# First tile's weight sums ahead of the norm, its stream sums on VectorE, modulation rows in halves with buffers of their own, and the feed-forward groups as 4 4 3 3 4 4

## The chip, the cores and the metric

The kernel runs on one core of a Trainium2 chip. The metric is the device time of one execution in microseconds, and of a kernel its median over several runs. The kernel before took 1985.98 us (three runs, 1985.26 to 1990.08).

The engines are named as in the profile: PE is TensorE (PEld its weight loads), DVE is VectorE, ACT is ScalarE, POOL is GpSimd, and SP is SyncE, whose queue issues nearly all transfers. Each engine works through its own list of instructions in order, and waits at an instruction until the semaphores it needs have come.

## The reference, cut to what matters

Two layers of a transformer trunk over 512 latent and 256 context tokens, width 1024, all in float32. Layer 0 is differential attention beside a gated DeltaNet, layer 1 neighbourhood attention. Each layer ends with a SwiGLU feed-forward block, and each half of a layer starts with an RMS norm that is modulated by rows computed from the conditioning vectors:

```python
m = silu_c @ ada_w[l] + ada_b[l]                      # 6 rows of 1024: shifts, scales, gates
hf = rms_norm(x, norm_ffn[l]) * (1.0 + sc_f) + sh_f   # the norm ahead of the feed-forward block
x = x + g_f * swiglu(hf, ffn_w_in[l], ffn_w_out[l])   # silu(h @ w_gate) * (h @ w_up) @ w_out
```

The hidden width is 2816, or 22 tiles of 128. The change is in the feed-forward block of layer 0 (768 tokens) and in the two norms around it. While that block runs, the kernel also computes the modulation rows of layer 1.

## The kernel before, in words

**Precision.** Every float32 product is three TensorE passes. An operand is split in two parts, `hi` (ACT rounds it, `ACTIVATE`) and `lo` (DVE subtracts, `TENSOR_TENSOR`), and `mm3` (L180) adds hi·hi, hi·lo and lo·hi in one PSUM bank.

**The block upwards.** Gate and up product of a hidden tile are computed together by Strassen's scheme in Winograd's form: seven products in place of eight, over the two halves of the 1024 input rows and over gate and up as the two halves of the columns. That needs sums of blocks on both sides.

On the weight side, `weights(t)` (L1503) loads the tile's gate part `g` and up part `u` (512 KB each) into the staging ring `st` (two buffers for the whole kernel, `wstage`), and POOL forms four sums in two buffers `ws` (L1508, L1509, L1512, L1513). ACT and DVE split `g`, the two sums and the last block `a22` (L1499, L1500).

On the stream side, the sums are formed once, by the norm object `NormS`. Its method `finish` normalises a third of the tokens (context, then two halves of the latents), `put` writes `hf`, and `half` forms the sums. `half(0)` splits `b11` and `b21`, which need only the first two thirds. `half(1)` forms T1 and T2 on DVE (L414, L416) and T3 and T4 on POOL (L420, L423), and splits these and `b22` (L399, L400).

For each tile `up` runs `b11`, `b21`, then T2, T1, then T3, `b22`, then T4: seven times twelve passes of 384 columns, 84 in all. It ends with `emit`, which writes the tile `mid`.

**The block downwards.** After each group of tiles (`GROUPS0`: 4 4 4 4 3 3), `down` multiplies the group's `mid` tiles with the output weights, one output channel tile after the other (eight, called channels below): a load of 256 KB (for four tiles), a split (L166, L167), and 24 passes per channel for a group of four, half of 256 and half of 512 columns, and two updates of `x` on DVE (L1579). In the last group, five of the channels are done third by third, so that the next norm can start on the first third. `mid` has five buffers, shared with the four `hf`.

**The modulation rows.** `ada_rows` (L277) computes three blocks of sixteen row sums. Per row tile it loads 512 KB through the same ring `st`, and DVE multiplies with a row of silu(c) and sums (L286): two instructions of 512 columns, and in the first block four, since it serves latents and context. One step (`ada_step`) is a row tile. It is called once a channel, and before every second tile from the second group on.

**The norm.** `acc` squares a channel tile on ACT (L322) and adds it to a running sum (L324). Tiles from `on_v` on are added on DVE, the others on POOL. `NORMS` has 5 for the norm ahead of this block (`n0f`) and 8 for the one behind it (`n1m`), that is, all on POOL. `finish` adds over partitions on PE (`sp`, L335), takes the inverse root in some fourteen small instructions (`rsqrt`, L194 to L206, nearly all on POOL), spreads it over the partitions on PE (`rb`, L341), and scales on DVE (L344).

**What sets the order.** The program is written in one sequence, and a scheduler lays it out on the engines by its own estimate of times. The order of an engine is therefore not that of the text.

Of the kernel before, what the change touches and what calls it, by code (L numbers as in the profile page):

```python
# [22 lines left out]
GROUPS = [(0, 6), (6, 5), (11, 6), (17, 5)]  # L23
GROUPS0 = [(0, 4), (4, 4), (8, 4), (12, 4), (16, 3), (19, 3)]
HALF = 384
# [8 lines left out]
ORDER = "vp0 out1 Ad0 Bd1 vp1 Bd2 Bd3 Ad1 Ad2 G2 G0 Ad3 G1 G3".split()  # L34
NORMS = dict(n0f=(5, 'G', (7,)), n1m=(8, 'G', (7,)), n1f=(4, 'G', ()))
FILL = dict(out1=2, Ad0=1, vp1=2, Ad2=1, G2=3, Ad3=1, G1=3)
# [90 lines left out]
def build(tc, a, out, dbg=None):  # L127
# [3 lines left out]
    with es:  # L131
# [145 lines left out]
        def ada_rows(l, b, ns, stage, cbc, junk):  # L277
            lab(f"ada{l}{b}")
            sc = ct(f"scal{l}{b}", [128, 2, 16])
            part = ct("adpart", [128, 2, 2, 16])  # L280
            for j in range(16):
                st = stage(a["ada_t"][l, 16 * b + j], 1024)
                for s in range(ns):
                    for i in range(2):
                        cs = slice(512 * i, 512 * i + 512)
                        r = V.scalar_tensor_tensor(  # L286
                            out=junk() if s < ns - 1 else st[:, cs], in0=st[:, cs], scalar=1.0, in1=cbc[:, s, cs],
                            op0=ALU.mult, op1=ALU.mult, accum_out=part[:, s, i, j:j + 1],
                        )
                        tc.add_manual_dep(r.ins, last_lo[0].name, after, reason="pace")  # L290
                yield 0, 0
            for s in range(ns):
                V.tensor_tensor(out=sc[:, s, :], in0=part[:, s, 0, :], in1=part[:, s, 1, :], op=ALU.add)
                V.tensor_tensor(out=sc[:, s, :], in0=sc[:, s, :], in1=ada_b[:, l, 16 * b:16 * b + 16], op=ALU.add)
            ada_names(l, b, sc, ns)
            yield 0, 0
# [65 lines left out]
        class NormS(Norm):  # L362
# [12 lines left out]
            def put(self, k, s, sl, t):  # L375
                if self.hf is None:
                    self.hf = [self.fp.tile([128, 2, 2, HALF], F32, name="hf", tag="mid", bufs=5) for _ in range(4)]
                d = self.hf[k // 2][:, k % 2]
# [24 lines left out]
            def half(self, i):  # L403
# [3 lines left out]
                if i == 0:  # L407
# [3 lines left out]
                    return  # L411
                t1 = [self.fp.tile([128, 1024], F32, name="t1", tag="ws", bufs=2)[:, 0:2 * HALF].rearrange("p (z n) -> p z n", z=2) for _ in range(2)]
                for q in range(2):
# [4 lines left out]
                for q in range(2):  # L418
                    self.split("T1", q, t1[q])
                    G.tensor_tensor(out=b(0, 1, q), in0=b(1, 1, q), in1=b(0, 1, q), op=ALU.subtract)  # L420
                for q in range(2):
                    self.split("T3", q, b(0, 1, q))
                    G.tensor_tensor(out=b(1, 0, q), in0=b(1, 0, q), in1=b(0, 0, q), op=ALU.subtract)  # L423
                for q in range(2):
# [196 lines left out]
def l0_mixer(kx, hi, lo, xes):  # L621
# [799 lines left out]
    kx.fp0 = kx.fpx.enter_context(tc.tile_pool(name="fp0", bufs=1))  # L1421
    kx.n0 = kx.NormS(x, 0, "f", kx.np, kx.gs, SEGS, kx.fp0)
    for q, (s, sl) in enumerate(SEGS):
        lab("out2")
# [43 lines left out]


def ffn0(kx, x, nm, next_norm):  # L1470
    tc, nc, a = kx.tc, kx.nc, kx.a
# [7 lines left out]
    with kx.fpx:  # L1479

        def adas():
            cbc = fp.tile([128, 2, 1024], F32, name="cbc", tag="cbc", bufs=1)
            DMA.dma_start(out=cbc, in_=a["cbc"])
            S.activation(out=cbc, in_=cbc, func=AF.Silu)
            junk = lambda: gs.tile([128, 512], F32, name="junk", tag="C")
            for b in range(3):
                yield from kx.ada_rows(1, b, 1 if b else 2, kx.wstage, cbc, junk)

# [14 lines left out]
        def weights(t):  # L1503
            g, u = (kx.wstage(a["wfi"][0, t, z], 1024) for z in range(2))
            a11, a12, a21, a22 = g[:, 0:512], g[:, 512:1024], u[:, 0:512], u[:, 512:1024]
            yield split(g, 1024)
            sa = fp.tile([128, 1024], F32, name="ws", tag="ws", bufs=2)
            G.tensor_tensor(out=sa[:, 0:512], in0=a21, in1=a22, op=ALU.add)  # L1508
            G.tensor_tensor(out=sa[:, 512:1024], in0=sa[:, 0:512], in1=a11, op=ALU.subtract)  # L1509
            yield split(sa, 1024)  # L1510
            sb = fp.tile([128, 1024], F32, name="ws", tag="ws", bufs=2)
            G.tensor_tensor(out=sb[:, 0:512], in0=a11, in1=a21, op=ALU.subtract)  # L1512
            G.tensor_tensor(out=sb[:, 512:1024], in0=a12, in1=sa[:, 512:1024], op=ALU.subtract)  # L1513
            yield split(sb, 1024)
            yield split(a22, 512, ("a22h", "a22l"))

# [65 lines left out]

        for gi, (t0, ng) in enumerate(GROUPS0):
            mids = [fp.tile([128, 2, 2, HALF], F32R, name="mid", tag="mid", bufs=5) for _ in range(ng)]
            for t in range(t0, t0 + ng):
                if gi and t % 2:
                    ada_step()
                lab(f"ffi0{gi}")
                for _ in up(t, mids[t - t0]):
                    pass  # L1590
            tail = 5 if gi == len(GROUPS0) - 1 else 0
# [365 lines left out]
```

## Time and profile before

| what | value |
|---|---|
| median of three runs | 1985.98 us |
| the profiled execution: its own time, its span | 1987.38 us, 1985.6 us |
| mean granted TensorE clock | 0.961 |
| PE busy | 1807.4 us, 91% of the span |
| DVE, ACT, POOL busy | 1239.4, 805.1, 380.0 us |
| the block of layer 0 with the norm behind it | 693 to 1300 us of the span |

Times in the profile count from the span's start. A row of a group view reads: line, engine, operation, output and inputs, shape, count, then busy time in us and mean duration in ns, then the engine's idle time just before these instructions and what ended it. A row of a timeline reads: start and duration in us, engine, line, operation, and in brackets the idle time before it with what ended it. A row of a table of stretches gives for each engine its busy time and, in brackets, the number of instructions, then the granted clock, the share of DMA engines that were busy and GB/s.

### The profile page before, as it was taken

How to read it: one execution, taken by the hardware profiler on the slowest of the kernel's cores; microseconds unless marked ns; L12 is line 12 of the kernel's file. 1: busy time of each engine (PE TensorE's matmuls, PEld its weight loads, DVE VectorE, ACT ScalarE, POOL GpSimd, SP SyncE). 2: the span in 40 equal slices, each digit the busy share in tenths (PEclk: the TensorE clock that was granted, in tenths of full speed). 3: DMA queues.
4: the chain of work that ended last, by engine and by line, in shares of the span. 5: the costliest groups of instructions: out<-in, count | busy, mean ns of one | idle time of the engine just before them, and what ended most of it. 6: DMA issues, size and time to landing. Idle time of an engine off the chain costs nothing.

```text
span 1985.6 us, 30314 instructions
## 1 busy us (share of the span) xinstructions
PE 1807.4 (91%) x11328; PEld 1625.1 (82%) x11328; DVE 1239.4 (62%) x2826; ACT 805.1 (41%) x1773; POOL 380.0 (19%) x449
## 2 busy tenths in 40 slices
PE   5978999798989939899999998889999989999999
PEld 3867889677878839798989897879999778888887
DVE  6556688776676677777767776656565663434333
ACT  3434554345664453141424232445555442222221
POOL 2132314431210063030413113321101020000000
PEclk8978999899999969999999999989999989999999
DMA  7556645647444602323243433311211213323232
GB/s 293 154 177 208 195 140 153 185 136 218 112 153 130 222 13 81 120 98 126 96 149 101 144 108 115 106 40 57 69 55 45 79 33 106 106 77 114 85 107 94
DMA packets 107522, 238.41 MB, mean 120 GB/s; under 512 B 11152, under 2 KB 50320, under 8 KB 106224
## 3 DMA queue, kind: packets, MB, share of 16 engines
q1 hardware_dynamic: 94848, 208.31, 32.9%
q0 software_dynamic: 4064, 14.38, 2.5%
q10 hardware_dynamic: 8464, 13.79, 2.0%
q8 instruction: 89, 1.46, 0.3%
q14 instruction: 57, 0.47, 0.1%
HBM read 203.44 MB, written 32.99 MB: 119 GB/s over the span
## 4 chain that ended last, share of the span: by engine, by line
PE 56%; DVE 15%; DMA 14%; POOL 5%; ACT 4%; issue 4%; SPq 0%; POOLq 0%; ACTq 0%; DVEq 0%
PE f L180 25%; PE d L180 17%; DMA st<-in_ada_t_dram 4%; DMA qkd<-ar 3%; PE o L180 3%; DMA st<-in_wfi_dram 2%; DVE st L286 2%; DVE wlo L1500 1%; PE vp L547 1%; PE sc L1762 1%; POOL ws L1508 1%; PE o L1787 1%; POOL ws L1512 1%; DVE ev L1536 1%; POOL ws L1509 1%
## 5 line engine op out<-in xcount | busy, mean ns | idle before, releaser
L166 ACT ACTIVATE whi<-st 128x1024 fp32r<-128x1024 f32 (+6 forms) x191 | 170.1, 892 | 451.7 <-PE f L180 195.6
L167 DVE TENSOR_TENSOR wlo<-st,whi 128x1024 fp32r<-128x1024 f32 (+6 forms) x191 | 196.4, 1029 | 158.3 <-ACT whi L166 155.8
L180 PE MATMUL d<-whi,hhi 128*128 128x256 f32 (+1 forms) x800 | 235.3, 296 | 20.1 <-ACT ar L211 13.3
L180 PE MATMUL d<-wlo,hhi 128*128 128x256 f32 (+1 forms) x800 | 233.3, 292 | 1.3 <-DVE wlo L167 1.3
L180 PE MATMUL d<-whi,hlo 128*128 128x256 f32 (+1 forms) x800 | 233.0, 293 | 0.2 <-DVE hlo L357 0.2
L180 PE MATMUL f<-hhi,whi 128*128 128x512 f32 (+2 forms) x632 | 229.6, 364 | 1.7 <-ACT hhi L356 1.0
L180 PE MATMUL f<-hlo,whi 128*128 128x512 f32 (+2 forms) x632 | 230.0, 364 | 0.2 <-DVE hlo L357 0.2
L180 PE MATMUL f<-hhi,wlo 128*128 128x512 f32 (+2 forms) x632 | 227.6, 362 | 0.0
L180 PEld LDWEIGHTS d<-whi,hhi 128*128 128x128 f32 x800 | 157.3, 197 | 26.4 <-ACT ar L211 14.6
L180 PE MATMUL f<-mid,whi 128*128 128x512 f32 (+1 forms) x644 | 159.0, 343 | 6.8 <-ACT whi L166 5.8
L180 PE MATMUL f<-v,whi 128*128 128x384 f32 x528 | 138.8, 344 | 27.1 <-ACT whi L1499 24.5
L180 PEld LDWEIGHTS d<-wlo,hhi 128*128 128x128 f32 x800 | 157.6, 197 | 2.5 <-DVE wlo L167 1.7
L180 PEld LDWEIGHTS d<-whi,hlo 128*128 128x128 f32 x800 | 157.0, 197 | 1.6 <-DVE hlo L357 0.4
L180 PEld LDWEIGHTS f<-hhi,whi 128*128 128x128 f32 x632 | 119.9, 190 | 15.8 <-ACT whi L1499 1.5
L180 PEld LDWEIGHTS f<-hlo,whi 128*128 128x128 f32 x632 | 120.3, 190 | 13.8 <-DVE hlo L357 0.5
L180 PEld LDWEIGHTS f<-hhi,wlo 128*128 128x128 f32 x632 | 119.7, 190 | 13.1
L180 PEld LDWEIGHTS f<-mid,whi 128*128 128x128 f32 x644 | 109.4, 192 | 23.8 <-ACT whi L166 9.8
L180 PEld LDWEIGHTS f<-v,whi 128*128 128x128 f32 x528 | 97.9, 194 | 30.3 <-ACT whi L1499 26.9
L180 PE MATMUL d<-hhi,whi 128*128 128x512 f32 (+1 forms) x304 | 107.9, 355 | 3.1 <-ACT cin L211 1.4
L180 PE MATMUL f<-mid,wlo 128*128 128x256 f32 (+1 forms) x322 | 106.1, 343 | 5.1 <-DVE wlo L167 5.0
L1508 POOL TENSOR_TENSOR ws<-st 128x512 f32<-128x512 f32 x22 | 32.5, 1476 | 383.3 <-DMA st<-in_wfi_dram 296.2
L180 PE MATMUL d<-hlo,whi 128*128 128x512 f32 (+1 forms) x304 | 105.8, 348 | 0.0
(410 smaller groups left out, 4319.6 us busy)
## 6 DMA issues: line engine op xcount, KB each, us to landing
st<-in_wfi_dram SPq DMA_DIRECT2D x88, 512.0 KB, 3.3
st<-in_ada_t_dram SPq DMA_DIRECT2D x48, 512.0 KB, 3.3
st<-in_ada_w_dram SPq DMA_DIRECT2D x32, 512.0 KB, 4.2
aw<-in_ada_dram SPq DMA_DIRECT2D x8, 1024.0 KB, 12.6
st<-in_wfo_dram SPq DMA_DIRECT2D x32, 256.0 KB, 3.4
st<-in_w1kv_dram SPq DMA_DIRECT2D x16, 512.0 KB, 3.2
aqT<-qkd SPq DMA_DIRECT2D x48, 128.0 KB, 3.2
st<-in_wfo_dram SPq DMA_DIRECT2D x16, 384.0 KB, 3.0
```

Of the source, the lines that this page charges most:

```text
L166: S.activation(out=hi, in_=st, func=AF.Copy)
L167: last_lo[:] = [V.tensor_tensor(out=lo, in0=st, in1=hi.bitcast(F32), op=ALU.subtract).ins]
L180: r = T.matmul(out=ps, lhsT=p, rhs=q, start=(c == 0), stop=(c == n - 1))
L286: r = V.scalar_tensor_tensor(out=junk() if s < ns - 1 else st[:, cs], in0=st[:, cs], scalar=1.0, in1=cbc[:, s, cs], op0=ALU.mult, op1=ALU. ...
L547: T.matmul(out=vp[i, s], lhsT=w[:, ws], rhs=h[k][:, sl], start=(k == 0 and q == 0), stop=(k == KT - 1 and q == 2),)
L1500: kx.last_lo[:] = [V.tensor_tensor(out=lo, in0=src, in1=hi.bitcast(F32), op=ALU.subtract).ins]
L1508: G.tensor_tensor(out=sa[:, 0:512], in0=a21, in1=a22, op=ALU.add)
L1509: G.tensor_tensor(out=sa[:, 512:1024], in0=sa[:, 0:512], in1=a11, op=ALU.subtract)
L1512: G.tensor_tensor(out=sb[:, 0:512], in0=a11, in1=a21, op=ALU.subtract)
L1536: V.tensor_tensor(out=out, in0=ps, in1=sb, op=ALU.add)
L1762: T.matmul(out=o, lhsT=lq[:, q], rhs=kv(lk), start=(i == 0), stop=(i == 2))
L1787: T.matmul(out=o, lhsT=lv[:, v, :], rhs=p, start=(n == 0 and i == 0), stop=(n == 5 and i == 2))
```

## The change

- **Weight sums of the first tile.** A new function `prep` holds the loads and the four POOL sums. For tile 0 it is called before the norm's loop and the result kept in `kx.prep0`. In group 0, the first part of tiles 0 and 1 (`b11`, `b21`) is recorded ahead of the rest of both.
- **Stream sums on VectorE.** T3 and T4 go from POOL to DVE. The buffer of T1 is no longer taken from `ws` but from that of the row `cbc`.
- **Modulation rows in halves.** A step is half a row tile (256 KB), and goes through a ring of its own, `ast`, with three buffers. Steps are taken after the first and second part of a tile from tile 2 on (in the last three groups after all three parts), and once a channel as before.
- **Norm behind the block.** `n1m` has 5 for 8: channel tiles 5, 6 and 7 are added on DVE.
- **Groups** 4 4 3 3 4 4, and four `mid` buffers for five.

```diff
-GROUPS0 = [(0, 4), (4, 4), (8, 4), (12, 4), (16, 3), (19, 3)]
+GROUPS0 = [(0, 4), (4, 4), (8, 3), (11, 3), (14, 4), (18, 4)]
-NORMS = dict(n0f=(5, 'G', (7,)), n1m=(8, 'G', (7,)), n1f=(4, 'G', ()))
+NORMS = dict(n0f=(5, 'G', (7,)), n1m=(5, 'G', (7,)), n1f=(4, 'G', ()))
...
             for j in range(16):
-                st = stage(a["ada_t"][l, 16 * b + j], 1024)
-                for s in range(ns):
-                    for i in range(2):
-                        cs = slice(512 * i, 512 * i + 512)
+                for i in range(2):
+                    cs = slice(512 * i, 512 * i + 512)
+                    st = stage(a["ada_t"][l, 16 * b + j, :, cs], 512)
+                    for s in range(ns):
...
-                yield 0, 0
+                    yield 0, 0
...
-                t1 = [self.fp.tile([128, 1024], F32, name="t1", tag="ws", bufs=2)[:, 0:2 * HALF].rearrange("p (z n) -> p z n", z=2) for _ in range(2)]
+                t1 = self.fp.tile([128, 2, 2, HALF], F32, name="t1", tag="cbc", bufs=1)
+                t1 = [t1[:, q] for q in range(2)]
...
-                    G.tensor_tensor(out=b(0, 1, q), in0=b(1, 1, q), in1=b(0, 1, q), op=ALU.subtract)
+                    V.tensor_tensor(out=b(0, 1, q), in0=b(1, 1, q), in1=b(0, 1, q), op=ALU.subtract)
...
-                    G.tensor_tensor(out=b(1, 0, q), in0=b(1, 0, q), in1=b(0, 0, q), op=ALU.subtract)
+                    V.tensor_tensor(out=b(1, 0, q), in0=b(1, 0, q), in1=b(0, 0, q), op=ALU.subtract)
...
     kx.n0 = kx.NormS(x, 0, "f", kx.np, kx.gs, SEGS, kx.fp0)
+    kx.prep0 = prep(kx, 0)
...
+def prep(kx, t):
+    G = kx.nc.gpsimd
+    g, u = (kx.wstage(kx.a["wfi"][0, t, z], 1024) for z in range(2))
+    a11, a12, a21, a22 = g[:, 0:512], g[:, 512:1024], u[:, 0:512], u[:, 512:1024]
+    sa, sb = (kx.fp0.tile([128, 1024], F32, name="ws", tag="ws", bufs=2) for _ in range(2))
+    G.tensor_tensor(out=sa[:, 0:512], in0=a21, in1=a22, op=ALU.add)
+    G.tensor_tensor(out=sa[:, 512:1024], in0=sa[:, 0:512], in1=a11, op=ALU.subtract)
+    G.tensor_tensor(out=sb[:, 0:512], in0=a11, in1=a21, op=ALU.subtract)
+    G.tensor_tensor(out=sb[:, 512:1024], in0=a12, in1=sa[:, 512:1024], op=ALU.subtract)
+    return g, u, sa, sb
...
+            def astage(src, n):
+                st = fp.tile([128, n], F32, name="ast", tag="ast", bufs=3)
+                DMA.dma_start(out=st, in_=src)
+                return st
+
             for b in range(3):
-                yield from kx.ada_rows(1, b, 1 if b else 2, kx.wstage, cbc, junk)
+                yield from kx.ada_rows(1, b, 1 if b else 2, astage, cbc, junk)
...
         for gi, (t0, ng) in enumerate(GROUPS0):
-            mids = [fp.tile([128, 2, 2, HALF], F32R, name="mid", tag="mid", bufs=5) for _ in range(ng)]
-            for t in range(t0, t0 + ng):
-                if gi and t % 2:
-                    ada_step()
-                lab(f"ffi0{gi}")
-                for _ in up(t, mids[t - t0]):
-                    pass
+            mids = [fp.tile([128, 2, 2, HALF], F32R, name="mid", tag="mid", bufs=4) for _ in range(ng)]
+            ups = [up(t, mids[t - t0]) for t in range(t0, t0 + ng)]
+            lab(f"ffi0{gi}")
+            if gi == 0:
+                for u in ups[0:2]:
+                    next(u)
+            for i, u in enumerate(ups):
+                for j, _ in enumerate(u):
+                    if t0 + i > 1 and (j or gi > 2):
+                        ada_step()
+                        lab(f"ffi0{gi}")
```

Where the scheduler puts it shows at three places. Up to the norm ahead of the block and behind the one after it, the lists of all engines are the same as before.

**POOL, around the norm ahead of the block.** `ssq` are the running sums of squares of the three thirds, `rs_y` and `rs_t` the inverse root, `ws` the weight sums, `st` the staged weights. Before, the four sums of tile 0 stand behind the last inverse root and among the stream sums:

```order
L206 TENSOR_TENSOR rs_y_7782<-rs_y_7782,rs_t_7783 128x2
L420 TENSOR_TENSOR hf_7511<-hf_7513,hf_7511 128x2x384
L420 TENSOR_TENSOR hf_7512<-hf_7514,hf_7512 128x2x384
L423 TENSOR_TENSOR hf_7513<-hf_7513,hf_7511 128x2x384
L1508 TENSOR_TENSOR ws_7920<-st_7883 128x512
L423 TENSOR_TENSOR hf_7514<-hf_7514,hf_7512 128x2x384
L1512 TENSOR_TENSOR ws_7956<-st_7881,st_7883 128x512
```

Now they stand at the head of the list, among the first squares, and two of tile 1's (`ws_7929`) inside the first third's inverse root:

```order
L1477 TENSOR_TENSOR ws_7400<-st_7398 128x512
L1479 TENSOR_TENSOR ws_7401<-st_7396,st_7398 128x512
L324 TENSOR_TENSOR ssq0_7414<-ssq0_7414,sq_7424 128x256
L1478 TENSOR_TENSOR ws_7400<-ws_7400,st_7396 128x512
L324 TENSOR_TENSOR ssq0_7414<-ssq0_7414,sq_7435 128x256
L1480 TENSOR_TENSOR ws_7401<-st_7396,ws_7400 128x512
```

```order
L206 TENSOR_TENSOR rs_y_7498<-rs_y_7498,rs_t_7499 128x2
L1477 TENSOR_TENSOR ws_7929<-st_7927 128x512
L200 TENSOR_TENSOR rs_t_7499<-rs_y_7498 128x2
L324 TENSOR_TENSOR ssq2_7708<-ssq2_7708,sq_7729 128x256
L1478 TENSOR_TENSOR ws_7929<-ws_7929,st_7925 128x512
L201 TENSOR_TENSOR rs_t_7499<-rs_t_7499,rs_v_7500 128x2
```

`ws_7929` takes the buffer of `ws_7400`, so it is written only after DVE has split that one.

**SP, the loads of the first group's channels.** `in_ada_t` are the modulation rows, `in_wfo` the output weights. Before, both take turns in `st`:

```order
L160 DMA st<-in_ada_t_dram 128x1024
L160 DMA st<-in_wfo_dram 128x512
L160 DMA st<-in_ada_t_dram 128x1024
L160 DMA st<-in_wfo_dram 128x512
L160 DMA st<-in_ada_t_dram 128x1024
```

Now the rows are half as long and go to `ast`, and `st` is left to the weights:

```order
L1503 DMA ast<-in_ada_t_dram 128x512 x2
L160 DMA st<-in_wfo_dram 128x512
L1503 DMA ast<-in_ada_t_dram 128x512
L160 DMA st<-in_wfo_dram 128x512
L1503 DMA ast<-in_ada_t_dram 128x512 x2
```

**POOL, the norm behind the block.** Before, the last squares of the second and third thirds stand between the steps of the first third's inverse root:

```order
L198 TENSOR_SCALAR rs_v_12735<-ms_12731 128x2
L324 TENSOR_TENSOR ssq1_12530<-ssq1_12530,sq_12854 128x256
L197 TENSOR_SCALAR rs_y_12733<-rs_y_12733 128x2
L324 TENSOR_TENSOR ssq2_12532<-ssq2_12532,sq_12927 128x256
L200 TENSOR_TENSOR rs_t_12734<-rs_y_12733 128x2
L324 TENSOR_TENSOR ssq2_12532<-ssq2_12532,sq_12941 128x256
L201 TENSOR_TENSOR rs_t_12734<-rs_t_12734,rs_v_12735 128x2
```

Now the first root runs through, and what is left of the squares follows it:

```order
L198 TENSOR_SCALAR rs_v_12815<-ms_12811 128x2
L197 TENSOR_SCALAR rs_y_12813<-rs_y_12813 128x2
L200 TENSOR_TENSOR rs_t_12814<-rs_y_12813 128x2
L201 TENSOR_TENSOR rs_t_12814<-rs_t_12814,rs_v_12815 128x2
L205 TENSOR_SCALAR rs_t_12814<-rs_t_12814 128x2
```

On PE, the first third's `sp` stood 27 passes of the block ahead of the end, and no pass stood between `rb` of the first third and `rb` of the second. Now 75 passes follow `sp`, 55 of them ahead of the first `rb` and 20 between the first and the second.

More of the change, by code (lines that the diff above doesn't have):

```diff
@@ L281, in ada_rows @@
             for j in range(16):
-                st = stage(a["ada_t"][l, 16 * b + j], 1024)
-                for s in range(ns):
-                    for i in range(2):
-                        cs = slice(512 * i, 512 * i + 512)
+                for i in range(2):
+                    cs = slice(512 * i, 512 * i + 512)
+                    st = stage(a["ada_t"][l, 16 * b + j, :, cs], 512)
+                    for s in range(ns):
                         r = V.scalar_tensor_tensor(
-                            out=junk() if s < ns - 1 else st[:, cs], in0=st[:, cs], scalar=1.0, in1=cbc[:, s, cs],
+                            out=junk() if s < ns - 1 else st, in0=st, scalar=1.0, in1=cbc[:, s, cs],
                             op0=ALU.mult, op1=ALU.mult, accum_out=part[:, s, i, j:j + 1],
@@ L376, in put @@
                 if self.hf is None:
-                    self.hf = [self.fp.tile([128, 2, 2, HALF], F32, name="hf", tag="mid", bufs=5) for _ in range(4)]
+                    self.hf = [self.fp.tile([128, 2, 2, HALF], F32, name="hf", tag="mid", bufs=4) for _ in range(4)]
                 d = self.hf[k // 2][:, k % 2]
@@ L1503, in weights @@
         def weights(t):
-            g, u = (kx.wstage(a["wfi"][0, t, z], 1024) for z in range(2))
-            a11, a12, a21, a22 = g[:, 0:512], g[:, 512:1024], u[:, 0:512], u[:, 512:1024]
+            g, u, sa, sb = kx.prep0 if t == 0 else prep(kx, t)
             yield split(g, 1024)
-            sa = fp.tile([128, 1024], F32, name="ws", tag="ws", bufs=2)
-            G.tensor_tensor(out=sa[:, 0:512], in0=a21, in1=a22, op=ALU.add)
-            G.tensor_tensor(out=sa[:, 512:1024], in0=sa[:, 0:512], in1=a11, op=ALU.subtract)
             yield split(sa, 1024)
-            sb = fp.tile([128, 1024], F32, name="ws", tag="ws", bufs=2)
-            G.tensor_tensor(out=sb[:, 0:512], in0=a11, in1=a21, op=ALU.subtract)
-            G.tensor_tensor(out=sb[:, 512:1024], in0=a12, in1=sa[:, 512:1024], op=ALU.subtract)
             yield split(sb, 1024)
-            yield split(a22, 512, ("a22h", "a22l"))
+            yield split(u[:, 512:1024], 512, ("a22h", "a22l"))
         cnt = [0]
```

## The prediction

> **What bounds the kernel now.** I read the page first, for the engine that bounds:
>
> ```profile
> PE 1807.4 (91%) x11328; PEld 1625.1 (82%) x11328; DVE 1239.4 (62%) x2826; ACT 805.1 (41%) x1773; POOL 380.0 (19%) x449
> ```
>
> PE does, so an edit is worth the PE time without progress that it removes. The lists of all engines differ only from the norm ahead of layer 0's feed-forward block to the norm behind it. So I cut that part, 693 to 1300 us, at its stages: norm, then upward and downward passes of each group in turn, then norm.
>
> ```profile
> core 0: us, PE busy (x) PEld busy (x) DVE busy (x) ACT busy (x) POOL busy (x), PEclk, DMA share, GB/s
> 693.00:742.40 49.40, 17.88 (x100) 16.27 (x99) 38.49 (x59) 29.49 (x60) 31.64 (x58) 0.69 0.03 11
> 742.40:799.10 56.70, 56.15 (x313) 55.33 (x314) 44.95 (x74) 21.23 (x31) 17.91 (x13) 0.97 0.25 81
> 799.10:840.20 41.10, 35.49 (x193) 28.60 (x192) 29.82 (x75) 5.90 (x9) 0.00 (x0) 1.00 0.40 133
> 840.20:903.10 62.90, 60.80 (x337) 59.83 (x338) 47.99 (x88) 22.70 (x34) 22.46 (x16) 0.97 0.28 93
> 903.10:943.00 39.90, 37.09 (x194) 31.50 (x193) 28.30 (x71) 7.02 (x11) 0.50 (x1) 0.91 0.39 132
> 943.00:1002.80 59.80, 58.87 (x338) 58.24 (x337) 42.11 (x72) 22.46 (x33) 20.46 (x16) 1.00 0.34 109
> 1002.80:1036.90 34.10, 33.70 (x194) 29.32 (x193) 24.21 (x53) 6.89 (x11) 0.32 (x1) 1.00 0.46 149
> 1131.10:1175.40 44.30, 43.98 (x253) 43.64 (x252) 31.17 (x58) 16.44 (x25) 13.98 (x11) 1.00 0.34 109
> 1175.40:1208.10 32.70, 27.15 (x146) 21.34 (x144) 23.44 (x54) 5.51 (x10) 0.00 (x0) 1.00 0.46 149
> 1208.10:1255.50 47.40, 46.19 (x252) 45.23 (x253) 32.42 (x56) 18.36 (x28) 16.19 (x12) 0.96 0.29 92
> 1278.90:1300.40 21.50, 7.65 (x47) 7.27 (x47) 8.57 (x23) 8.56 (x22) 14.48 (x39) 0.65 0.09 26
> ```
>
> The same work takes unequal times. Four tiles upwards cost 59.8 us at best (336 passes, 0.178 us each) and 62.9 in the second group. Eight channels downwards cost 34.1 us at best (4.26 a channel), but 41.1 and 39.9 in the first two groups. In the fifth group, three tiles need 44.3 us upwards, and downwards 32.7, where three quarters of 34.1 are 25.6; the sixth needs 47.4 upwards. The two norms take 49.4 and 21.5 us with little on PE.
>
> **Part 1: modulation rows.** The waits for PE and the transfers in the first group's channels:
>
> ```profile
> 790.64 3.31 DMA st<-in_ada_t_dram
> 797.00 3.34 DMA st<-in_ada_t_dram
> 803.90 3.44 DMA st<-in_ada_t_dram
> PE f L180 <- ACT whi L166: 5.8, 7, 1.2
> st<-in_ada_t_dram SPq DMA_DIRECT2D x7, 512.0 KB, 3.4
> st<-in_wfo_dram SPq DMA_DIRECT2D x8, 256.0 KB, 3.5
> L286 DVE SCALAR_TENSOR_TENSOR junk<-st,cbc 128x512 f32<-128x512 f32 x12 | 8.1, 717 | 4.7 <-DMA st<-in_ada_t_dram 4.7
> L286 DVE SCALAR_TENSOR_TENSOR st<-st,cbc 128x512 f32<-128x512 f32 x12 | 7.9, 688 | 0.0
> L1579 DVE SCALAR_TENSOR_TENSOR x<-f,scal,x 128x512 f32<-128x512 f32 x7 | 5.2, 746 | 0.0
> L167 DVE TENSOR_TENSOR wlo<-st,whi 128x512 fp32r<-128x512 f32 x6 | 4.1, 688 | 0.1
> L1579 DVE SCALAR_TENSOR_TENSOR x<-f,scal,x 128x256 f32<-128x256 f32 x8 | 3.8, 480 | 3.6 <-PE f L180 3.6
> L166 ACT ACTIVATE whi<-st 128x512 fp32r<-128x512 f32 x6 | 3.8, 632 | 26.3 <-DMA st<-in_wfo_dram 17.6 <-PE f L180 8.7
> ```
>
> A row tile starts every 6.4 to 6.9 us: 3.3 to 3.4 of landing, then two products of 717 and two of 688 ns before its buffer is free, 6.2 in all. Output weights take turns with it in the same queue, so they come at that pace, against PE's 4.26 a channel. PE lives off its three split buffers and then waits.
>
> Now `st` holds weights alone. A buffer turns in 3.5 + 0.63 + 0.69 = 4.8 us, two give a load every 2.4. A half row turns in 3.5 + 1.4 = 4.9, three give one every 1.6. VectorE needs 0.69 + 0.48 + 0.75 + 1.4 = 3.3 us a channel. All are under 4.26, so PE bounds again. The excess over the best is 41.1 − 34.1 = 7.0; 62.9 − 59.8 = 3.1; 39.9 − 34.1 = 5.8; 32.7 − 25.6 = 7.1; 47.4 − 44.3 = 3.1: **26.1 us**. The new order of groups is the same sum of parts.
>
> Not all comes back. I leave 1 us for each of five turns between groups, where the first load upwards still follows the last output weights, and 2 for the upward passes: the second group takes eight half steps for two whole ones, four more of 1.4 us on VectorE, 47.99 + 5.6 = 53.6 of 59.8. Gain **19**, bounds 8 (VectorE holds PE up) and 26. `mid` with four buffers costs nothing: the first write into a new one follows 60 passes (10.7 us) behind the last reader on PE. If that cover were gone, the price is those passes once a group.
>
> A rule of the Trainium skill speaks against halves: "DMA: Bandwidth & Descriptors", section "Rules for kernel authors", asks for transfers of 1 MiB and more. The rows bear it out in part, 256 KB landing no sooner than 512 (3.5 and 3.4 us). By that rule the sum would lose this part and more; its rival stands below.
>
> **Part 2: the norm ahead of the block and the first tiles.**
>
> ```profile
> 689.72 1.28 ACT L1484 ACT_TABLE_LOAD   x1
> 691.14 1.91 ACT L1484 ACTIVATE cbc<-cbc 128x2048 f32<-128x2048 f32 x1
> 693.44 1.56 POOL L324 TENSOR_TENSOR ssq<-ssq,sq 128x256 f32<-128x256 f32 x2 [5.05 <-ACT sq L322]
> 702.75 0.71 PE L341 MATMUL rb<-cst,rs_y 128*128 128x128 f32 x4 [3.02 <-POOL rs_y L206]
> 718.62 1.22 PE L341 MATMUL rb<-cst,rs_y 128*128 128x128 f32 x4 [1.77 <-POOL rs_y L206]
> 729.51 0.95 DVE L400 TENSOR_TENSOR hlo<-hf,hhi 128x768 fp32r<-128x768 f32 x1
> 730.38 2.56 DVE L400 TENSOR_TENSOR hlo<-t,hhi 128x768 fp32r<-128x768 f32 x1
> 739.30 1.97 POOL L1509 TENSOR_TENSOR ws<-ws,st 128x512 f32<-128x512 f32 x1
> 742.42 1.01 PE L180 MATMUL f<-v,whi 128*128 128x384 f32 x2 [18.56 <-ACT whi L1499]
> 752.26 1.29 POOL L1509 TENSOR_TENSOR ws<-ws,st 128x512 f32<-128x512 f32 x1
> ```
>
> PE stands 18.6 us for the split of tile 0's first sum, which POOL finishes at 739.30 + 1.97. That wait goes, but what is late next is the norm. POOL gets six sums ahead of the first `rb`: four of tile 0, two of tile 1, at 1.3 (alone) to 2.0 us (beside VectorE), 8 to 12 us. Its idle time there was 5.0 in one gap, mostly from the Silu of `cbc` with its table load (3.2 us on ACT), which moves away; the gap is now filled. Net 3 to 7 us late. Worse, tile 1's first sum stands in the first third's root and needs the buffer that VectorE frees; by the order of VectorE's list that split follows the last squares, at about 703. I take 7 (first `rb` from 702.8 to 710), and with the same steps behind it the last one too (725.6).
>
> Behind the last `rb`, VectorE has eight scalings (0.42 us, as L344 has it below), eight subtractions and eight low parts (0.95) and, by the sizes, two weight splits of some 1.2 and three updates of 0.55: 3.4 + 15.2 + 2.4 + 1.7 = 22.7 us. Before, low parts that stood beside POOL's sums took up to 2.56 in place of 0.95. With 3 us for tile 1's other two POOL sums, which still stand beside VectorE here, it ends near 725.6 + 1.2 + 22.7 + 3 = 752.5.
>
> PE, however, has more to do meanwhile: 24 passes of tile 0 and 24 of tile 1, then those of the next products whose operands are split by 753, by the order of VectorE's list some 54. That is 102. Before it had 24 and those from 742.4 on, at 0.178 and with some 2.5 us lost to half clock (10.6 − 2.5 = 8.1 us, or 45). The 33 more are worth 5.9; I take **3** off, for half clock over the longer norm: gain **3**, bounds −6 (a later norm, nothing gained on PE) and +10 (norm not late).
>
> **Part 3: the norm behind the block.**
>
> ```profile
> 1274.08 7.88 POOL L324 TENSOR_TENSOR ssq<-ssq,sq 128x256 f32<-128x256 f32 x9 [0.39 <-ACT sq L322]
> 1289.53 1.22 PE L341 MATMUL rb<-cst,rs_y 128*128 128x128 f32 x4 [6.71 <-POOL rs_y L206]
> 1290.79 1.66 DVE L344 SCALAR_TENSOR_TENSOR nt<-x,gain,rb 128x256 f32<-128x256 f32 x4 [7.45 <-PE rb L341]
> 1298.10 1.22 PE L341 MATMUL rb<-cst,rs_y 128*128 128x128 f32 x4 [6.70 <-POOL rs_y L206]
> 1279.30:1282.90 3.60, 3.48 (x27) 1.00 0.02 5
> ```
>
> POOL adds squares at 0.88 us each, and five of them stand in the first root. Nine of 21 go to VectorE. From `sp` (1278.9) to the next layer's first pass (1300.4) PE had 27 passes, 3.5 us, in 21.5. Now 75 follow `sp`, at 0.12 to 0.13 some 9 us. The first root loses five adds (3.7 us of 10.7) and lies behind 55 passes; from `rb` to `rb` stay 8.6 and 2.3 behind the last. So 7 + 8.6 + 2.3 = 17.9, of which 9 are work: 18.0 idle become 8.9. Gain **9**, bounds 4 (VectorE, or four halves left over, delays the first root) and 11.
>
> **Sum.** 19 + 3 + 9 = 31, from 1987.4 us of the profiled execution to 1956.4. The median of the runs shown is 1.4 lower, so **1955 us**.
>
> **The rivals.**
>
> - *All of it.* The norm isn't late, no turn costs anything: 26 + 10 + 11 = 47, 1939 us. For it: POOL's idle time nearly covers the sums of tile 0. Against: a shared buffer in the root.
> - *The first norm costs more than its wait.* −6 in place of +3, with 15 and 8 of the others: 17, 1969 us. For it: tile 1's sums in POOL's list. Against: 24 more passes of cover.
> - *VectorE takes PE's place upwards.* 53.6 of 59.8 us, in order, beside POOL. If each of six upward stretches grows by 5 us, the 31 are gone: 1986 us. Against: the rows' half steps leave a tenth free, and PSUM holds several products.
> - *Halves cost as much as wholes.* The mechanism is the transfer itself. If output weights and a half land one after the other in the queue, 3.5 + 3.4 = 6.9 us a channel against 4.26, then 43 channels pay 2.6 each, 114, and lose the 19: 1986 + 114 − 12 = 2088 us. It decides from 0.7 us a channel (31 / 43). Against: 1002.8 to 1036.9 moves both, with whole rows, in 4.26 a channel, so transfers overlap. This is the skill's rule on small transfers as this kernel would pay it.
>
> **How the numbers follow.** A difference of 0.3%, 6 us, is about what the measurement can tell from none. Forecast 0.52, all of it 0.13, a dearer first norm 0.19, VectorE 0.09, halves 0.07. The first three are faster: 0.84; same 0.09; slower 0.07. Range of the forecast alone: 1945 to 1965 (8 to 26 of part 1 hardly meets the extremes of the others). To leave out no more than 2 in 10 it goes from 1939 to the dearer norm with some of part 1 lost as well: 1939 to 1975.
>
> **What would show it.** Right: channels downwards at 4.3 us from the first group on, no wait for L166 or L167 above 1 us; the wait of 18.6 us gone; passes between `sp` and `rb` behind the block. Wrong: `rb` of the first norm later than 713; VectorE over nine tenths busy upwards with PE waiting for PSUM; half rows that land later than VectorE wants them.

## The result, and the profile after

The changed kernel takes **1937.86 us** (median of four runs, 1937.32 to 1938.9) beside 1988.01 of the kernel before on the same chip: ratio **0.9749, 95% interval 0.9732 to 0.9766**, or 50 us gained (47 to 53). The forecast was 1955 with a range of 1939 to 1975. The sign was right. The gain was forecast at 31 us and measured at 50, and the time lies 1 us beyond the range. The profiled execution took 1938.09 us (span 1936.3), 49.3 less than before.

The page after, its busy times and the shares of its chain of waits:

```profile
PE 1794.5 (93%) x11343; PEld 1623.0 (84%) x11343; DVE 1257.4 (65%) x2839; ACT 805.2 (42%) x1773; POOL 380.5 (20%) x436
PE 72%; DVE 6%; DMA 5%; ACT 3%; POOL 2%; issue 2%; SPq 0%; POOLq 0%; ACTq 0%; DVEq 0%
```

The stretches of the block after, cut as the prediction cut them before: end of the products ahead of the norm to the last `rb`, the rest of the first group's upward passes, then downward and upward in turn, and the last group's channels in two pieces at `sp`:

```profile
core 0: us, PE busy (x) PEld busy (x) DVE busy (x) ACT busy (x) POOL busy (x), PEclk, DMA share, GB/s
700.70:727.55 26.85, 8.91 (x35) 7.92 (x35) 14.19 (x31) 14.05 (x32) 16.96 (x47) 0.62 0.00 1
727.55:796.30 68.75, 61.03 (x326) 57.99 (x325) 65.90 (x100) 33.82 (x51) 16.91 (x10) 0.95 0.24 77
796.30:829.70 33.40, 33.40 (x193) 29.46 (x193) 26.70 (x57) 8.14 (x12) 6.06 (x4) 1.00 0.46 142
829.70:888.00 58.30, 58.30 (x338) 58.27 (x337) 52.18 (x102) 22.91 (x34) 17.84 (x12) 1.00 0.35 113
921.40:965.10 43.70, 43.70 (x253) 43.66 (x253) 37.15 (x76) 16.80 (x25) 13.50 (x8) 1.00 0.31 103
965.10:990.30 25.20, 25.20 (x147) 22.14 (x145) 18.51 (x37) 5.39 (x9) 3.58 (x3) 1.00 0.43 136
1209.10:1234.30 25.20, 25.20 (x179) 23.68 (x178) 19.48 (x41) 12.40 (x26) 7.70 (x9) 1.00 0.51 157
1234.30:1252.20 17.90, 12.34 (x97) 12.05 (x95) 13.02 (x36) 8.73 (x23) 11.32 (x34) 0.87 0.10 30
```

From 796 to 1234 us PE is busy for the whole of every stretch. Eight channels take 33.4 us in the first group already (41.1 before), four tiles upwards 58.3 (62.9 and 59.8 before), three tiles 43.7 and 25.2 (44.3 and 32.7). The waits of PE from 772 to 1249 us come to one, at the very edge. A row of waits reads: who waited for what, then us in total, how often, and the longest. (L1519 and L1520 of the changed kernel are L1499 and L1500 of the kernel before.)

```profile
PE f L180 <- DVE wlo L1520: 1.0, 1, 1.0
```

From 799 to 1278 us before, they were these:

```profile
PE f L180 <- ACT whi L1499: 6.3, 7, 2.4
PE f L180 <- ACT whi L166: 5.8, 7, 1.2
PE f L180 <- DVE wlo L167: 5.0, 5, 1.6
PE f L180 <- DVE wlo L1500: 2.2, 6, 0.6
PE f L180 <- ACT mid L1541: 0.8, 2, 0.4
```

Those 20.1 us are waits alone, and the stretches were longer than after by more. In the second group's channels (903 to 943 us, mean granted clock 0.91) a lowered clock makes up most of the rest, as the last section shows. The first group's channels were 7.7 us longer than after at a clock of 1.00, with 5.1 us of waits; what the other 2.6 are is not shown.

The norm ahead of the block, PE's first work after idle time:

```profile
710.07 1.22 PE L341 MATMUL rb<-cst,rs_y 128*128 128x128 f32 x4 [9.37 <-POOL rs_y L206]
717.29 1.22 PE L341 MATMUL rb<-cst,rs_y 128*128 128x128 f32 x4 [5.36 <-POOL rs_y L206]
727.07 0.71 PE L341 MATMUL rb<-cst,rs_y 128*128 128x128 f32 x4 [0.93 <-POOL rs_y L206]
741.38 0.44 PE L180 MATMUL f<-hhi,a22h 128*128 128x384 f32 x1 [1.28 <-ACT hhi L399]
743.77 0.69 PE L180 MATMUL f<-hlo,whi 128*128 128x384 f32 x1 [1.96 <-DVE hlo L400]
```

The wait of 18.6 us is gone. In its place the three `rb` come 7.3 to 8.5 us later than before (6.3 to 7.5 from the end of the products ahead, which itself came 1.0 later), and small waits for the splits on ACT and VectorE follow. The upward passes of the first group end at 796.3 (before 799.1).

### The profile page after: what moved, and what is told of

It reads as the page before. It is cut to its first block, busy times and chain, and to the rows that moved or that the text cites. A ratio compares the mean times of both kernels' runs of the same rounds, so it can differ in the third digit from the quotient of the medians.

```text
span 1936.3 us, 30405 instructions
## 1 busy us (share of the span) xinstructions
PE 1794.5 (93%) x11343; PEld 1623.0 (84%) x11343; DVE 1257.4 (65%) x2839; ACT 805.2 (42%) x1773; POOL 380.5 (20%) x436
## 4 chain that ended last, share of the span: by engine, by line
PE 72%; DVE 6%; DMA 5%; ACT 3%; POOL 2%; issue 2%; SPq 0%; POOLq 0%; ACTq 0%; DVEq 0%
PE f L180 43%; PE d L180 16%; PE o L180 3%; DMA qkd<-ar 1%; PE sc L1779 1%; PE o L1804 1%; PE m L954 1%; PE S L1250 1%; PE t L1278 1%; DMA st<-in_ada_w_dram 1%; PE m L1793 1%; DVE e L1264 0%; PE m L1052 0%; PE m L1750 0%; PE m L1066 0%
## 5 line engine op out<-in xcount | busy, mean ns | idle before, releaser
L180 PE MATMUL f<-mid,whi 128*128 128x512 f32 (+1 forms) x624 | 151.5, 337 | 0.0
L180 PE MATMUL d<-hhi,wlo 128*128 128x512 f32 (+1 forms) x304 | 105.5, 348 | 0.0
```

The lines of the kernel that those rows point to most:

```text
L180: r = T.matmul(out=ps, lhsT=p, rhs=q, start=(c == 0), stop=(c == n - 1))
```

## The experiments

All times are medians; each ratio is to the kernel before on the same chip. Microseconds gained are (1 − ratio) × 1988.

### Part 1 by itself

Four edits of the kernel before take the modulation rows apart, and a fifth run repeats the last of them in the changed kernel. The first is the kernel before with that part of the change alone (steps placed as in the change, four `mid` buffers):

```diff
-                st = stage(a["ada_t"][l, 16 * b + j], 1024)
+                for i in range(2):
...
+                    st = stage(a["ada_t"][l, 16 * b + j, :, cs], 512)
...
+                st = fp.tile([128, n], F32, name="ast", tag="ast", bufs=3)
-                yield from kx.ada_rows(1, b, 1 if b else 2, kx.wstage, cbc, junk)
+                yield from kx.ada_rows(1, b, 1 if b else 2, astage, cbc, junk)
```

> The kernel before with part 1 alone: modulation rows in halves, three buffers of their own, steps placed as in the change, four `mid` buffers; groups, both norms and the first tile as before. As the prediction had it (26 us of excess over the best stages, 7 of them kept): gain 19, 1969 us. If the rows slowed every stage between the first group's channels and the norm behind the block, the best ones too, and no turn keeps anything: gain 36, about 1952 us, four tiles upwards in 58.4 us and eight channels in 33.5 from the first group on. If the better pace of the changed kernel came from its groups or its first tile: at most 26, 1962 us or more, and four tiles upwards still 59.8.

Measured: 1952.16 us, ratio 0.9819 (0.98 to 0.9839): **36 us** (32 to 40), against 19 of the prediction. Two stretches of the first and second group:

```profile
797.10:830.55 33.45, 33.45 (x194) 29.48 (x194) 24.27 (x49) 6.86 (x10) 6.54 (x4) 1.00 0.40 122
830.55:888.80 58.25, 58.25 (x337) 58.25 (x336) 51.81 (x102) 23.08 (x34) 18.08 (x12) 1.00 0.35 113
```

This is the pace of the changed kernel, with the groups and the first tile of before. The better pace is the rows' doing.

PE waits for nothing in that kernel from 797 to 1241 us.

The second keeps whole row tiles at their old places and gives them two buffers of their own (four `mid` buffers make room):

```diff
+                st = fp.tile([128, n], F32, name="ast", tag="ast", bufs=2)
...
-                yield from kx.ada_rows(1, b, 1 if b else 2, kx.wstage, cbc, junk)
+                yield from kx.ada_rows(1, b, 1 if b else 2, astage, cbc, junk)
```

> The kernel before, its row tiles whole as they were and at their old places, but through two buffers of their own (four `mid` buffers make room). If it is the shared buffers that cost: weights alone turn in 3.5 + 0.63 + 0.69 = 4.8 us, two buffers give one every 2.4; whole rows turn in 3.4 + 2.8 = 6.2, two give one every 3.1; both under 4.2, so nearly the whole gain of part 1, 1950 to 1958 us. If it is the halving (finer pieces of VectorE's work and of the queue): little gain, 1978 us or more.

Measured: 1953.34 us, ratio 0.9823 (0.9794 to 0.9851): 35 us (30 to 41). Whole rows gain as much as halves, within some 5 us. What counts is the ring, not the size of the pieces. A shared ring with more buffers was not tried: the runs do not tell a ring apart from more buffers in all (two before, four here, five in the change).

The third is its mirror, halves at the steps of the change, through the shared ring. Its edit against the first of these kernels:

```diff
-                yield from kx.ada_rows(1, b, 1 if b else 2, astage, cbc, junk)
+                yield from kx.ada_rows(1, b, 1 if b else 2, kx.wstage, cbc, junk)
```

> Modulation rows in halves with steps placed as in the change, but through the two shared buffers; otherwise the kernel before. If the shared buffers cost: a half (3.5 + 1.4) and an output weight (4.8) in turn through two buffers allow a channel each 4.85 us against 4.2, and before it was (6.2 + 4.8) / 2 = 5.5; the channels keep two thirds of their waits, and upwards the halves stand in the way of the tiles' loads: gain 5 to 15, 1973 to 1983 us. If the halving does it: 1950 to 1958 us.

Measured: 2012.34 us, ratio 1.0113 (1.0074 to 1.0152), 22 us **slower**, which neither theory had. The rows are three stretches (the first group's channels, the second group's upward passes, and the last group's channels with the norm), then the waits of PE from the first group's channels to the norm, and the loads in the upward stretch (count, KB each, us to landing):

```profile
804.00:838.80 34.80, 34.10 (x193) 29.28 (x194) 25.19 (x56) 7.06 (x11) 0.00 (x0) 1.00 0.43 135
838.80:907.70 68.90, 63.19 (x338) 61.05 (x337) 54.77 (x95) 22.03 (x33) 23.62 (x16) 0.95 0.27 88
1272.25:1329.05 56.80, 33.64 (x210) 29.75 (x209) 34.69 (x75) 22.16 (x50) 25.80 (x50) 0.81 0.35 108
```

```profile
PE f L180 <- ACT whi L1499: 15.6, 12, 2.3
PE f L180 <- ACT whi L166: 7.6, 8, 2.0
PE f L180 <- ACT v L166: 7.1, 2, 6.1
PE f L180 <- DVE wlo L1500: 5.0, 9, 1.1
```

```profile
st<-in_wfi_dram SPq DMA_DIRECT2D x6, 512.0 KB, 3.8
st<-in_ada_t_dram SPq DMA_DIRECT2D x10, 256.0 KB, 2.5
```

In the upward stretch ten halves take turns in two buffers, where before five whole rows did: the same bytes in twice the turns. Each half landed sooner (2.5 us against 3.4), and still the stretch grew from 62.9 to 68.9. In the trace the waits moved mostly to L1499 and L1500, the splits of the next upward weights. Downwards it was the other way. There one half takes the turn of one whole row, and the first group's channels took 34.8 us in place of 41.1. Over the block the channels of the first five groups got about 11 us shorter, the upward passes about 23 longer, and the last group with its norm 12 longer (56.8 for 44.9); six halves were loaded beside the last group's channels, and none before. So in a shared ring both the number of turns and the length of each counted. The edit moves the steps as well, so the 22 us are not the price of halving alone.

The fourth leaves the rows out, so layer 1 is modulated by the biases alone:

```diff
-            for j in range(16):
+            V.memset(part, 0.0)
+            for j in range(0):
```

> The kernel before without the loads and products of layer 1's modulation rows (left out: so layer 1 is modulated by the biases alone). All that the rows cost. If they slowed even the best stages: four tiles upwards in 58.3 to 58.5 us in every group, eight channels in 33.5, about 1952 us or a little less. If the best stages of before were held by something else (the turn, the work on VectorE): upwards stays at 59.8, channels at 34.1, 1962 us.

Measured: 1952.1 us, ratio 0.9817 (0.98 to 0.9835): 36 us.

```profile
799.50:832.95 33.45, 33.45 (x194) 29.50 (x193) 17.87 (x27) 6.70 (x10) 6.52 (x4) 1.00 0.27 80
832.95:891.20 58.25, 58.25 (x338) 58.25 (x337) 38.73 (x59) 23.06 (x35) 18.26 (x12) 1.00 0.20 64
```

So 36 us is all that the rows cost in the kernel before, and a ring of their own returns it whole. The same edit in the changed kernel asks whether anything is left:

> The changed kernel without the loads and products of layer 1's modulation rows (left out: so layer 1 is modulated by the biases alone). If its rows cost nothing any more: 1938 us. If the 7 us that the prediction kept for turns and for VectorE upwards were there after all, or VectorE's half steps still hold PE at places that no wait shows: 1931 us.

Measured: 1939.01 us, ratio 0.974 (0.9716 to 0.9763), the changed kernel's own within the interval. Its rows are free; the 7 us kept back were not there.

### Part 2 by itself

The kernel before, with tile 0's sums ahead of the norm, the first part of tiles 0 and 1 first, and T3 and T4 on VectorE:

```diff
+    kx.prep0 = prep(kx, 0)
...
-                    G.tensor_tensor(out=b(0, 1, q), in0=b(1, 1, q), in1=b(0, 1, q), op=ALU.subtract)
+                    V.tensor_tensor(out=b(0, 1, q), in0=b(1, 1, q), in1=b(0, 1, q), op=ALU.subtract)
...
+                for u in ups[0:2]:
+                    next(u)
```

> The kernel before with part 2 alone: tile 0's sums ahead of the norm, first part of tiles 0 and 1 ahead of the rest, T3 and T4 on VectorE, T1 in the buffer of `cbc`; rows, groups and the other norm as before. By the prediction: gain 3, 1986 us (the wait of 18.6 us goes, the last `rb` comes some 7 us later). If the later norm costs more than the wait: 1995 us. If the part is worth what is left of the whole (50 less 37 of the rows less 9 of the norm behind): gain 4, 1985 us.

Measured: 1985.09 us, ratio 0.9983 (0.9966 to 0.9999): 3.4 us, as forecast, barely told from none. From the end of the products ahead of the norm to the end of the first group's upward passes, in the kernel before, this one and the changed kernel with the next edit:

```profile
699.70:799.10 99.40, 67.33 (x358) 65.07 (x358) 78.76 (x121) 46.67 (x79) 43.94 (x56) 0.83 0.16 52
```

```profile
703.60:800.60 97.00, 69.67 (x357) 65.62 (x358) 77.18 (x128) 48.48 (x83) 33.66 (x59) 0.86 0.15 50
```

```profile
704.90:797.10 92.20, 71.02 (x357) 67.76 (x358) 79.19 (x131) 48.78 (x84) 33.11 (x57) 0.83 0.18 58
```

The changed kernel takes 700.7 to 796.3 there, 95.6: part 2 alone shortens the stretch by 2.4 us, the whole change by 3.8. The third row is the changed kernel with tile 1's four POOL sums held behind the last root:

```diff
+    if t == 1:
+        kx.tc.add_manual_dep(r.ins, kx.last_root[0].name, kx.after, reason="pace")
```

> The changed kernel with tile 1's four POOL sums held behind the last root of the norm ahead of the block (two of them, 1.27 us each, stood in its first root). If they are what holds the norm: each `rb` 2.5 us sooner (first at 707.5), and 2 to 3 us gained, 1935 us. If the squares that also stand there hold it, or tile 1's splits now come late: no gain, 1938 us or more.

Measured: 1936.15 us, ratio 0.9731 (0.9705 to 0.9758). By the trace the stretch is 3.4 us shorter, and PE waits 6.63 us for the first `rb` against 9.37. The medians agree with that (1936.15 and 1937.86) and do not settle it; the profiled execution itself was 1.0 us longer than that of the change.

Next, on top of that edit, one root for both latent thirds, so that the last `rb` comes a whole chain sooner:

```diff
-        kx.n0.finish(q)
-        if q:
-            kx.n0.half(q - 1)
+        if q == 0:
+            kx.n0.finish(0)
+        if q == 2:
+            kx.n0.finish(1, 2)
+            kx.n0.half(0)
+            kx.n0.half(1)
```

> The changed kernel with tile 1's POOL sums behind the last root, and the two latent thirds of the norm ahead of the block in one root of four columns (one chain of some fourteen small POOL instructions, 7.2 us from `rb` to `rb`, in place of two). If the last `rb` is what the block's first products wait for: it comes 7 to 10 us sooner against the end of the products before, and 3 to 8 us are gained over the changed kernel, 1930 to 1935 us. If VectorE's 23 us of scalings, sums and splits behind it set the end, and only move together: up to 3 us, 1935 us or more.

Measured: 1933.58 us, ratio 0.9717 (0.9697 to 0.9737), the fastest kernel here; its interval meets that of the change. The rows: its second and last `rb`, the whole stretch up to the end of the first group's upward passes, and VectorE behind that `rb` (L343 there is L341 of the kernel before, and L404 below is L400):

```profile
715.78 2.08 PE L343 MATMUL rb<-cst,rs_y 128*128 128x128 f32 x8 [4.60 <-POOL rs_y L206]
```

```profile
700.10:792.10 92.00, 69.87 (x357) 65.94 (x358) 80.45 (x135) 48.28 (x83) 30.12 (x43) 0.87 0.19 62
717.89:748.30 30.41, 23.22 (x108) 20.39 (x109) 30.41 (x43) 24.67 (x39) 5.44 (x3) 0.88 0.15 52
```

The last `rb` now comes 15.7 us behind the products, 26.4 in the change (727.07 − 700.7). Yet the stretch is only 0.2 shorter than with tile 1's sums moved alone. VectorE is busy for all of 30.41 us behind that `rb`: the edit puts the scalings of both latent thirds and all splits behind it, so the earlier norm makes VectorE's queue longer. In the changed kernel it was busy for 23.08 of 23.10 us from 727.8, where the prediction had worked out 22.7 and 3. So the last `rb` by itself does not set the end. That VectorE's work does is read from its busy time; no kernel here gave it less to do.

The last edit gives T3 and T4 of that kernel back to POOL, which is idle there:

```diff
-                    V.tensor_tensor(out=b(0, 1, q), in0=b(1, 1, q), in1=b(0, 1, q), op=ALU.subtract)
+                    G.tensor_tensor(out=b(0, 1, q), in0=b(1, 1, q), in1=b(0, 1, q), op=ALU.subtract)
...
-                    V.tensor_tensor(out=b(1, 0, q), in0=b(1, 0, q), in1=b(0, 0, q), op=ALU.subtract)
+                    G.tensor_tensor(out=b(1, 0, q), in0=b(1, 0, q), in1=b(0, 0, q), op=ALU.subtract)
```

> The kernel with one root for the latent thirds, and its T3 and T4 (four subtractions of 0.95 us) back on POOL, which is idle for 21.6 us there; VectorE works without a gap from 717.9 to 748.3. If VectorE's own count of instructions sets the end: 3.8 us sooner, 1930 us. If a POOL sum holds VectorE up as before (a low part 2.56 in place of 0.95, a POOL sum 1.8): each of four costs VectorE the 0.95 it saved and 0.6 more, 1934 to 1937 us.

Measured: 1935.23 us, ratio 0.9727 (0.9702 to 0.9753): no difference. The rows are four low parts that start within a POOL sum, one (at 735.76) that starts just ahead of one, and two of POOL's sums:

```profile
725.32 2.54 DVE L404 TENSOR_TENSOR v<-hf,v 128x768 fp32r<-128x768 f32 x1
729.90 2.56 DVE L404 TENSOR_TENSOR hlo<-t,hhi 128x768 fp32r<-128x768 f32 x1
732.39 2.58 DVE L404 TENSOR_TENSOR hlo<-hf,hhi 128x768 fp32r<-128x768 f32 x1
735.76 0.94 DVE L404 TENSOR_TENSOR hlo<-hf,hhi 128x768 fp32r<-128x768 f32 x1
736.63 2.56 DVE L404 TENSOR_TENSOR hlo<-t,hhi 128x768 fp32r<-128x768 f32 x1
725.19 1.85 POOL L425 TENSOR_TENSOR hf<-hf 128x768 f32<-128x768 f32 x1 [8.85 <-ACT hf L387]
735.92 2.46 POOL L428 TENSOR_TENSOR hf<-hf 128x768 f32<-128x768 f32 x1 [1.77 <-DVE hf L421]
```

By these rows VectorE saved 4 × 0.95 = 3.8 us of subtractions and lost 4 × 1.6 = 6.4. The Trainium skill ("SBUF — State Buffer", section "SBUF: two separate sides") calls the pair of ports that VectorE and GpSimd share an exclusive lock, held for the whole instruction. The trace agrees: the sums end at 727.04 and 738.38, and the low parts that started within them at 727.86 and 739.19, 0.8 us later, nearly the whole 0.94 of one that is not held up. The low part at 735.76 began 0.16 us ahead of the sum and was not delayed; that sum took 2.46 us in place of 1.85.

### Part 3, and the groups

The kernel before with `n1m` 5 for 8 alone:

```diff
-NORMS = dict(n0f=(5, 'G', (7,)), n1m=(8, 'G', (7,)), n1f=(4, 'G', ()))
+NORMS = dict(n0f=(5, 'G', (7,)), n1m=(5, 'G', (7,)), n1f=(4, 'G', ()))
```

> The kernel before with part 3 alone: three of eight channel tiles of the norm behind the block squared into the sum on VectorE (`n1m` 5 for 8). By the prediction's working the first root loses five adds of 0.88, 3.7 us of 10.7, and more passes lie beside the root: 9 us, 1980 us (bounds 4 and 11). If the passes beside the root come from the last group of four tiles and not from this edit: 3 to 5 us, 1984 us.

Measured: 1984.92 us, ratio 0.9983 (0.9966 to 0.9999): 3.4 us, the second theory's size. The changed kernel with the groups of before:

```diff
-GROUPS0 = [(0, 4), (4, 4), (8, 3), (11, 3), (14, 4), (18, 4)]
+GROUPS0 = [(0, 4), (4, 4), (8, 4), (12, 4), (16, 3), (19, 3)]
```

> The changed kernel with the groups of before, 4 4 4 4 3 3. If the groups are the same sum of parts, as the prediction has it: 1938 us, no difference. If the last group of four is what covers the root behind the block (a third of its last five channels is 60 passes, of a group of three 45; 15 passes at 0.125 are 1.9 us, in two of the thirds): 1940 to 1942 us.

Measured: 1947.89 us, ratio 0.9791 (0.9764 to 0.9817), 8 us less gained than by the change (50 − 42), though the two intervals together leave room from about 2 to 15. Both theories had less (none, or 2 to 4). The changed kernel with all squares of that norm on POOL (the first edit of these three, turned round):

```diff
-NORMS = dict(n0f=(5, 'G', (7,)), n1m=(5, 'G', (7,)), n1f=(4, 'G', ()))
+NORMS = dict(n0f=(5, 'G', (7,)), n1m=(8, 'G', (7,)), n1f=(4, 'G', ()))
```

> The changed kernel with all squares of the norm behind the block added on POOL again (`n1m` 8). If the edits add up: 3 to 4 us slower, 1941.5 us. If the last group of four covers the first root by itself: no difference, 1938 us. If both are needed for the 9 us of part 3: up to 9 us slower, 1947 us.

Measured: 1940.31 us, ratio 0.9748 (0.9729 to 0.9767), no difference that can be told. From the start of the last group's downward passes to the first pass of the next layer, in order the kernel before, `n1m` alone, the changed kernel with the old groups, with POOL's squares, and as it is:

```profile
1255.50:1300.40 44.90, 30.24 (x211) 28.50 (x209) 24.71 (x53) 20.11 (x46) 23.95 (x50) 0.83 0.29 88
```

```profile
1257.00:1297.90 40.90, 29.39 (x211) 27.66 (x209) 27.75 (x61) 20.05 (x47) 18.25 (x41) 0.89 0.29 94
```

```profile
1214.35:1257.35 43.00, 29.93 (x210) 28.37 (x208) 31.81 (x75) 20.29 (x46) 19.27 (x41) 0.86 0.33 104
```

```profile
1207.10:1251.70 44.60, 37.41 (x274) 35.71 (x273) 29.05 (x65) 20.66 (x48) 24.16 (x50) 0.94 0.32 101
```

```profile
1209.15:1252.20 43.05, 37.49 (x273) 35.69 (x272) 32.45 (x76) 21.11 (x48) 19.02 (x42) 0.95 0.34 104
```

The last two hold 63 passes more, about 8.4 us of PE's work (a quarter of 33.45), in about the same time. With a last group of four, that tile's share of the downward work lies where PE stood for the norm. Why a group of three leaves only 16 passes behind `sp` and one of four leaves 75 was read and not tested. POOL first adds the squares of the first three channels, of all thirds, and only then those of the first third's other channels, on which `sp` waits. PE's passes of the first third end near 1229 us in both traces. POOL's first run ends at 1233.94 with the old groups, 4.9 us behind them, and at 1229.40 in the change, where the three channels ahead took PE longer:

```profile
1227.28 6.66 POOL L324 TENSOR_TENSOR ssq<-ssq,sq 128x256 f32<-128x256 f32 x7 [28.58 <-ACT sq L322]
```

```profile
1224.42 4.98 POOL L324 TENSOR_TENSOR ssq<-ssq,sq 128x256 f32<-128x256 f32 x6 [31.24 <-ACT sq L322]
```

## Why the prediction was right or wrong, point by point

**Part 1: the mechanism was right, the term was mis-sized, 19 for 36.** The rows' turns in the two-buffer ring shared with the weights were the cause, and PE does bound from the first group on. Of the 19 us between the forecast gain and the measured one, 17 lie here. Two steps failed.

- *"The excess over the best is ... 26.1 us."* The best stage of the kernel before was taken as free of the cause, and it wasn't. Every group had rows, and every turn went through the ring. The floor stood in the same trace, in any stretch in which PE didn't wait:

```profile
955.00:1000.00 45.00, 45.00 (x262) 45.00 (x261) 32.28 (x59) 18.48 (x28) 14.21 (x12) 1.00 0.30 95
1036.90:1096.80 59.90, 58.78 (x337) 58.14 (x336) 41.60 (x71) 22.63 (x34) 20.46 (x16) 1.00 0.33 106
1096.80:1131.10 34.30, 33.86 (x193) 29.44 (x193) 23.94 (x51) 7.08 (x11) 1.79 (x2) 1.00 0.43 138
```

The first row is within one upward stretch, 45.00 us and 262 passes, as dense as the stages after (58.30 and 338). Against 58.25 and 33.45 as floors (43.7 and 25.2 for three tiles) the five stages counted have 3.85 us more excess, and the five not counted have 5.3 (1.55, 0.65, 1.65, 0.85, 0.6). So 26.1 becomes 35.25; 36 was measured.

- *"I leave 1 us for each of five turns between groups ... and 2 for the upward passes."* Nothing of the 7 was there. The turns' waits (L1499, 6.3 us before) came from the ring too: with part 1 alone, the rows in a ring of their own, PE has none. VectorE at 52.18 of 58.30 us upwards, close to the 53.6 worked out, made PE wait for nothing; with whole rows in two buffers of their own it was busy for 56.87 of 58.55 us there, and PE for all of them.

"`mid` with four buffers costs nothing" held: PE waits for no `mid` in the trace after.

**Part 2: right, as far as 3 us can be told.** The first `rb` was put at 710 and came at 710.07, the last at 725.6 and came at 727.07. By 753 us PE was to have done 102 passes, and did some 103. The gain was put at 3 and measured 3.4 alone, 2.4 by that kernel's stretch and 3.8 by the changed kernel's. The step that named tile 1's sums in the first root is borne out by the 2.7 us that the first `rb` wins without them. That VectorE's work behind the last `rb` sets the end fits its busy time, and stays argued.

**Part 3: right in its sum, 9 for about 10, and in part by luck** (1.85 between the first and last of the five rows above, plus the 8.4 of the fourth tile's passes). `sp` to the first pass took 17.90, as worked out. One reading was off without effect: the trace before has six adds inside the first root, of 0.73 us, not five of 0.88; the 3.7 taken off is five of 0.73. The shares were off too. Of the 3.6 us by which `sp` to the first `rb` got shorter (10.66 to 7.03), 1.8 come back when all adds go to POOL again (8.83), and the time does not tell them. The sentence in part 1 that "the new order of groups is the same sum of parts" was wrong: the 75 passes behind `sp`, rightly counted here, come from the last group of four, and the edit of `n1m` alone brings 3.4, and nothing that can be told beside that group.

**The sum.** Alone, the parts gain 36 + 3.4 + 3.4, and the groups 8 in company: 51, against 50 for all.

**The rivals.** "All of it" (47, 1939 us, chance 0.13) came nearest, though its norm "isn't late" was wrong: the norm was late, and the rows gave more than 26. The dearer norm and VectorE in PE's place did not happen. "Halves cost as much as wholes", 6.9 us a channel, did not either: a channel took 4.2 (33.4 / 8), and halves and wholes in buffers of their own gained the same. The rule behind it (the Trainium skill, "DMA: Bandwidth & Descriptors", section "Rules for kernel authors", at least 1 MiB a transfer for the most bandwidth) found no measurable price here between 512 and 256 KB.

## What to carry to other kernels

Take the floor of a stage from the pace of a stretch without waits times its count of work, not from the best of its repetitions: if all of them share the suspected cause, the best one holds some of it too. Two streams of unequal urgency through one small ring held each other up; a ring apart for the one that can wait returned all of it, and the size of its pieces did not matter there. Within the shared ring it did: smaller pieces shortened the stages that kept their number of turns and lengthened those that doubled it. Where passes could be placed behind a serial chain, the size of the last group decided more than a faster chain did.

## What the runs showed of the hardware

- In the shared ring's upward stretch halves of 256 KB landed in 2.5 us, whole rows of 512 KB in 3.4, and yet the stretch took 6.0 us more with halves.
- A low part of VectorE that started within a POOL sum took 2.54 to 2.58 us and ended 0.8 behind the sum; one that started ahead of a sum took 0.94, and the sum was the longer one. These rows look as if whichever began later waited for the other's end, and was not slowed in part.
- A lowered granted clock adds to a stage what no wait shows. In the second group's channels before, PE's waits came to 2.8 us, and the stage was 6.45 over 33.45. Behind the longest of these waits, 1.56 us up to 924.03, the clock fell to 0.55 of full speed for seven microseconds. PE was busy for nearly all of them and got through 24 passes, against 43 in the next seven:

```profile
924.00:931.00 7.00, 6.97 (x24) 6.01 (x25) 4.13 (x13) 0.63 (x1) 0.00 (x0) 0.55 0.35 119
931.00:938.00 7.00, 7.00 (x43) 6.19 (x42) 4.67 (x14) 1.27 (x2) 0.00 (x0) 1.00 0.62 212
```

At the pace of the second row 24 passes take 3.9 us, so about 3 of the 6.45 are the clock.
